# LayerNorm with GELU: the rows of two buffers interleaved in HBM, partitions 64 KB apart instead of 32 KB

## The chip, the cores and the metric

The kernel runs on one core of one Trainium2 chip. The metric is the device time of one execution in microseconds (us); the median over runs is quoted. Runs of this kernel agree to about 0.2%. The profile shows the span of the core's work, which is 1.8 to 1.9 us shorter than the device time. MB and GB/s are in millions and billions of bytes, except where a transfer is called "4 MB": that is 4096 KB.

## The reference

```python
# x: (8, 1024, 2048) float32; gamma, beta: (2048,)
mean = np.mean(x, axis=-1, keepdims=True)
var = np.var(x, axis=-1, keepdims=True)
out = gamma * (x - mean) / np.sqrt(var + eps) + beta
return 0.5 * out * (1 + np.tanh(np.sqrt(2 / np.pi) * (out + 0.044715 * out ** 3)))
```

So 8192 rows of 8 KB go in and 8192 rows of 8 KB come out, 67.1 MB each way. Each row is worked on alone; which rows share a buffer is free to choose, as long as input and output agree.

## The kernel before

Rows go through five SBUF buffers of 128 partitions x 4 rows. The kernel makes 16 such groups: SyncE issues the loads, ScalarE the stores, and a load into a buffer waits until the store out of it has landed. VectorE computes statistics (L148) and the product with gamma (L164), ScalarE normalizes (L201) and does the GELU (L208), TensorE adds beta by matmuls into PSUM, GpSimd takes the power for the standard deviation.

```python
xg = xf.rearrange("(b p r) d -> b p r d", p=P, r=R)      # R = 4 rows, P = 128, 16 groups b
og = of.rearrange("(b p r) d -> b p r d", p=P, r=R)
...
for b in range(B):                                       # SyncE
    s = slot(b)
    if stored(b):
        sy.wait_ge(s_store[s], stored(b))                # the buffer's store has landed
    for q in range(R):
        if b == 0:                                       # first group: row by row
            sy.dma_start(out=xts[s][:, q:q + 1], in_=xg[0, :, q:q + 1]).then_inc(s_first[q], 16)
    if b:
        sy.dma_start(out=xts[s], in_=xg[b]).then_inc(s_load[s], 16)
...
ac.dma_start(out=og[b], in_=xt)._wait_ge(s_r, b + 1).then_inc(s_store[slot(b)], 16)   # ScalarE
# the last group is stored row by row (og[b, :, q:q + 1])
```

A group is one solid 4 MB of HBM: partition p has its 32 KB (4 rows), and the 32 KB of partition p + 1 follow at once.

Of the kernel before, what the change touches and what calls it, by code (L numbers as in the profile page):

```python
# [10 lines left out]
R = 4  # L11
# [5 lines left out]
def kernel(  # L17
# [9 lines left out]
    P = 128  # L27
    xf = x.flatten_outer_dims()
    of = out.flatten_outer_dims()
    n, d = xf.shape  # L30
# [3 lines left out]
    T = n // P  # L34
    B = T // R
    assert (B - 1) % SLOTS == 0
    xg = xf.rearrange("(b p r) d -> b p r d", p=P, r=R)
    og = of.rearrange("(b p r) d -> b p r d", p=P, r=R)

    bf16 = mybir.dt.bfloat16  # L40
    f32 = mybir.dt.float32
# [4 lines left out]
    def sb(name, shape, dt):  # L46
        return pool.tile(shape, dt, name=name)

    xts = [sb(f"xt{s}", [P, R, d], f32) for s in range(SLOTS)]
# [17 lines left out]
    def sem(name):  # L67
        return tc.alloc_semaphore(name)

    s_first = [sem(f"first{q}") for q in range(R)]  # L70
# [17 lines left out]
    def slot(b):  # L88
        return (b + SLOTS - 1) % SLOTS

    def row(p):
        return rows[p:p + 1, :, :d // K]

    def split(v):
        return v.rearrange("o (k f) -> o k f", k=K)
# [4 lines left out]
    def by_row(b):  # L100
        return b == B - 1

    def stored(b):
        return sum(16 * (R if by_row(c) else 1) for c in range(b) if slot(c) == slot(b))

    with tc.tile_critical(no_gpsimd_drain=True):  # L106
        with nc.Block(no_gpsimd_drain=True) as block:

            @block.sync
            def _(sy):  # L110
                for b in range(B):
                    s = slot(b)
                    if stored(b):
                        sy.wait_ge(s_store[s], stored(b))
                    for q in range(R):
                        if b == 0:
                            sy.dma_start(out=xts[s][:, q:q + 1], in_=xg[0, :, q:q + 1]).then_inc(s_first[q], 16)
                    if b:
                        sy.dma_start(out=xts[s], in_=xg[b]).then_inc(s_load[s], 16)

# [67 lines left out]
            @block.scalar  # L188
            def _(ac):
                ac.preload_act_table(ACT.Gelu_apprx_tanh)  # L190
                for k, (p, src) in enumerate(((64, gamma), (0, beta), (32, beta))):
                    ac.dma_start(out=row(p), in_=src.rearrange("(o k f) -> o k f", o=1, k=K)).then_inc(s_par[k], 16)
                ac.wait_ge(s_m, 1)
                ac.activation(out=split(b_hl[0:1]), in_=row(0), func=ACT.Identity)._wait_ge(s_par[1], 16).then_inc(s_c, 1)  # L194
                ac.activation(out=split(b_hl[32:33]), in_=row(32),  # L195
                              func=ACT.Identity)._wait_ge(s_par[2], 16).then_inc(s_c, 1)
                ac.activation(out=g_t, in_=pss[0], func=ACT.Identity)._wait_ge(s_tg, 1).then_inc(s_c, 1)  # L197
                for t in range(T + 1):
                    if t < T:
                        b, q = divmod(t, R)  # L200
                        ac.activation(out=yks[t % 2], in_=xts[slot(b)][:, q], func=ACT.Identity, scale=rss[:, q:q + 1],  # L201
                                      bias=nms[:, q:q + 1])._wait_ge(s_p, t + 1).then_inc(s_n, 1)
                    i = t - 1
                    if i < 0:
                        continue
                    b, q = divmod(i, R)
                    xt = xts[slot(b)]
                    ins = ac.activation(out=xt[:, q], in_=pss[i % 2], func=ACT.Gelu_apprx_tanh)._wait_ge(s_t, i + 1)  # L208
                    if by_row(b):
                        ins.then_inc(s_r, 1)  # L210
                        ac.dma_start(out=og[b, :, q:q + 1], in_=xt[:, q:q + 1])._wait_ge(  # L211
                            s_r, b + q + 1).then_inc(s_store[slot(b)], 16)
                        ac.sem_inc(s_g, 1)
                    elif q == R - 1:
                        ins.then_inc(s_r, 1)
                        ac.dma_start(out=og[b], in_=xt)._wait_ge(s_r, b + 1).then_inc(s_store[slot(b)], 16)  # L216
                        ac.sem_inc(s_g, 1)
                    else:
                        ins.then_inc(s_g, 1)
# [69 lines left out]
```

## Time and profile before

| | before |
|---|---|
| device time, median | 319.68 us |
| span in the profile | 317.8 us |
| busiest compute engine | VectorE, 265.0 us (83%) |
| the two DMA queues, share of 16 engines | 49.4% and 49.1% |
| bytes moved | 134.27 MB |
| rate in the middle of the run | 431 to 433 GB/s |

Read it in this order: no compute engine is full, the DMA engines are, and the stretch table shows whether their rate ever sags. The prediction below shows the lines.

### The profile page before, as it was taken

What the parts mean: (1) busy time and instruction counts of PE and PEld (TensorE: products, weight loads), DVE (VectorE), ACT (ScalarE), POOL (GpSimd) and SP (SyncE); (2) the same over time, 40 slices, a digit from 0 to 9 for tenths busy, and PEclk for the clock granted to TensorE, in tenths of its full rate; (3) what the DMA queues carried; (4) which work ended last, traced back from release to release, by engine and by line L of the source; (5) the groups of instructions that cost most, each with busy time, mean ns of one, the idle gap of its engine ahead of it and who ended that gap; (6) DMA issues with size and microseconds to landing.
All of it is one profiled execution on the core that took longest, in us unless ns stands there. A gap on an engine that the chain in (4) does not pass through costs nothing.

```text
span 317.8 us, 2075 instructions
## 1 busy us (share of the span) xinstructions
PE 244.3 (77%) x520; PEld 57.1 (18%) x520; DVE 265.0 (83%) x514; ACT 253.9 (80%) x132; POOL 79.0 (25%) x73
## 2 busy tenths in 40 slices
PE   2769988888888898888877868598595895868810
PEld 1211222111212122211111111122121111112100
DVE  3499999999999999999969799696996969879500
ACT  2679999999999999999969779696995969968920
POOL 1033323232323231323213222231312213212000
DMA  7999999999999999999999999999999999999994
GB/s 291 438 462 396 459 396 445 412 454 404 458 400 459 422 437 445 412 450 408 458 417 441 437 421 454 404 458 412 450 433 425 450 408 450 408 458 421 437 404 206
DMA packets 5571, 134.27 MB, mean 423 GB/s; under 512 B 656, under 2 KB 704, under 8 KB 704
## 3 DMA queue, kind: packets, MB, share of 16 engines
q1 hardware_dynamic: 2736, 67.11, 49.4%
q10 hardware_dynamic: 2832, 67.13, 49.1%
q14 instruction: 3, 0.02, 0.0%
HBM read 67.13 MB, written 67.11 MB: 422 GB/s over the span
## 4 chain that ended last, share of the span: by engine, by line
DMA 44%; DVE 27%; ACT 19%; PE 3%; issue 2%; ACTq 1%; DVEq 0%; SPq 0%
DMA out_dram<-xt 27%; DVE sts L148 15%; DMA xt<-in_x_dram 15%; ACT yk L201 12%; DVE zg L164 9%; ACT xt L208 7%; PE ps L226 2%; DMA rows<-in_gamma_dram 2%; DVE mvs L157 2%; DVE nms L141 1%; ACTq L216 1%; DVE ves L158 1%; PE ps L243 1%; ACT g_t L197 1%; ACTq L211 0%
## 5 line engine op out<-in xcount | busy, mean ns | idle before, releaser
L148 DVE BATCH_NORM_STATS2 sts<-xt 128x6 f32<-128x512 f32 x256 | 163.5, 681 | 23.7 <-DMA xt<-in_x_dram 21.7
L201 ACT ACTIVATE yk<-xt,nms,rss 128x2048 bf16<-128x2048 f32 x64 | 134.1, 2095 | 41.7 <-DVE nms L141 41.2
L243 PE MATMUL ps<-zg,ident 128*128 128x512 bf16 x256 | 120.8, 627 | 50.9 <-DVE zg L164 50.9
L132 POOL TENSOR_TENSOR rss<-ves,mhalf 128x1 f32<-128x1 f32 x64 | 78.0, 1219 | 216.5 <-DVE ves L158 157.0
L239 PE MATMUL ps<-b_hl,ones_b 33*128 33x512 bf16 x256 | 120.6, 624 | 2.2 <-PEq L234 2.2
L208 ACT ACTIVATE xt<-ps 128x2048 f32<-128x2048 f32 x64 | 118.8, 1857 | 1.5 <-PE ps L243 1.5
L164 DVE TENSOR_TENSOR zg<-yk,g_t 128x2048 bf16<-128x2048 bf16 x64 | 78.0, 1218 | 5.0 <-ACT yk L201 3.0
L243 PEld LDWEIGHTS ps<-zg,ident 128*128 128x128 bf16 x256 | 27.6, 130 | 144.1 <-DVE zg L164 108.7
L239 PEld LDWEIGHTS ps<-b_hl,ones_b 33*128 33x128 bf16 x256 | 27.0, 127 | 92.1 <-issue 88.4
L157 DVE BATCH_NORM_AGGREGATE mvs<-sts 128x2 f32<-128x24 f32 x64 | 16.9, 264 | 2.2
L141 DVE TENSOR_SCALAR nms<-mvs,rss 128x1 f32<-128x1 f32 x64 | 12.6, 196 | 0.0
L226 PE MATMUL ps<-rows,ones 1*128 1x512 f32 x8 | 7.2, 1072 | 6.0 <-DMA rows<-in_gamma_dram 6.0
L158 DVE TENSOR_SCALAR ves<-mvs 128x1 f32<-128x1 f32 x64 | 9.8, 154 | 2.2
L194 ACT ACTIVATE b_hl<-rows 1x2048 bf16<-1x2048 f32 x1 | 1.9, 1909 | 4.9 <-DMA rows<-in_beta_dram 4.9
L226 PEld LDWEIGHTS ps<-rows,ones 1*128 1x128 f32 x8 | 2.5, 323 | 9.2 <-DMA rows<-in_gamma_dram 6.0
L172 DVE TENSOR_TENSOR b_hl<-rows,b_hl 1x2048 bf16<-1x2048 f32 x1 | 2.3, 2281 | 2.1 <-ACT b_hl L195 2.1
L197 ACT ACTIVATE g_t<-ps 128x2048 bf16<-128x2048 f32 x1 | 1.9, 1877 | 2.4 <-PE ps L226 2.4
L190 ACT ACT_TABLE_LOAD x1 | 1.3, 1283 | 0.9 <-SPq L106 0.9
L167 DVE MEMSET b_hl<- 33x1024 uint32 x1 | 0.9, 912 | 1.2 <-SPq L106 1.2
L195 ACT ACTIVATE b_hl<-rows 1x2048 bf16<-1x2048 f32 x1 | 1.9, 1908 | 0.0
L123 POOL MEMSET ones<- 65x128 f32 x1 | 0.2, 202 | 0.5 <-SPq L106 0.5
L127 POOL TENSOR_SCALAR_AFFINE_SELECT ident<-ident 128x128 bf16<-128x128 bf16 x1 | 0.3, 294 | 0.1
(7 smaller groups left out, 0.9 us busy)
## 6 DMA issues: line engine op xcount, KB each, us to landing
xt<-in_x_dram SPq DMA_DIRECT2D x15, 4096.0 KB, 24.3
out_dram<-xt ACTq DMA_DIRECT2D x15, 4096.0 KB, 37.0
xt<-in_x_dram SPq DMA_DIRECT2D x4, 1024.0 KB, 8.1
out_dram<-xt ACTq DMA_DIRECT2D x4, 1024.0 KB, 12.7
rows<-in_beta_dram ACTq DMA_DIRECT2D x2, 8.0 KB, 5.6
rows<-in_gamma_dram ACTq DMA_DIRECT2D x1, 8.0 KB, 5.0
```

Of the source, the lines that this page charges most:

```text
L132: po.tensor_tensor(out=rss[:, c], in0=ves[:, c], in1=mhalf, op=ALU.pow)._wait_ge(s_a, k + 1).then_inc(s_q, 1)
L141: ve.tensor_scalar(out=nms[:, c], in0=mvs[:, q, 0:1], scalar1=rss[:, c], scalar2=-1.0, op0=ALU.mult, op1=ALU.mult)._wait_ge(s_q, count).th ...
L148: ins = ve.bn_stats(out=sts[:, q, j, :], in_=xr[:, j, :])
L157: ve.bn_aggr(out=mvs[:, q], in_=sts[:, q])._wait_ge(s_o, count + 1).then_inc(s_o, 1)
L158: ve.tensor_scalar(out=ves[:, q:q + 1], in0=mvs[:, q, 1:2], scalar1=float(eps), scalar2=1.0, op0=ALU.add, op1=ALU.mult)._wait_ge(s_o, coun ...
L164: ve.tensor_tensor(out=zgs[q % 2], in0=yks[q % 2], in1=g_t, op=ALU.mult)._wait_ge(s_n, count).then_inc(s_z, 1)
L197: ac.activation(out=g_t, in_=pss[0], func=ACT.Identity)._wait_ge(s_tg, 1).then_inc(s_c, 1)
L201: ac.activation(out=yks[t % 2], in_=xts[slot(b)][:, q], func=ACT.Identity, scale=rss[:, q:q + 1], bias=nms[:, q:q + 1])._wait_ge(s_p, t + ...
L208: ins = ac.activation(out=xt[:, q], in_=pss[i % 2], func=ACT.Gelu_apprx_tanh)._wait_ge(s_t, i + 1)
L226: ins = pe.matmul(pss[0][:, cols(j)], lhsT=ones[64:65], rhs=rows[64:65, j * K // nsub:(j + 1) * K // nsub, :d // K], start=True, stop=True)
L239: ins = pe.matmul(ps[:, cols(j)], lhsT=ones_b, rhs=b_hl[:, cols(j)], start=True, stop=False)
L243: ins = pe.matmul(ps[:, cols(j)], lhsT=ident, rhs=zgs[k % 2][:, cols(j)], start=False, stop=True)
```

## The change

The intent: let two consecutive groups share 8 MB of HBM. A partition owns eight consecutive rows (64 KB); the even group takes the first four, the odd group the last four. Each transfer still moves 128 runs of 32 KB, but they start 64 KB apart, so a transfer touches every second 32 KB of 8 MB.

```diff
-    xg = xf.rearrange("(b p r) d -> b p r d", p=P, r=R)
-    og = of.rearrange("(b p r) d -> b p r d", p=P, r=R)
+
+    def groups(v):
+        v = v.rearrange("(g p c r) d -> g c p r d", p=P, c=2, r=R)
+        return [v[b // 2, b % 2] for b in range(B)]
+
+    xg, og = groups(xf), groups(of)
...
-  ... in_=xg[0, :, q:q + 1]
+  ... in_=xg[0][:, q:q + 1]
...
-  ... out=og[b, :, q:q + 1]
+  ... out=og[b][:, q:q + 1]
```

More of the change, by code (lines that the diff above doesn't have):

```diff
@@ L116, in _ @@
                         if b == 0:
-                            sy.dma_start(out=xts[s][:, q:q + 1], in_=xg[0, :, q:q + 1]).then_inc(s_first[q], 16)
+                            sy.dma_start(out=xts[s][:, q:q + 1], in_=xg[0][:, q:q + 1]).then_inc(s_first[q], 16)
                     if b:
@@ L210, in _ @@
                         ins.then_inc(s_r, 1)
-                        ac.dma_start(out=og[b, :, q:q + 1], in_=xt[:, q:q + 1])._wait_ge(
+                        ac.dma_start(out=og[b][:, q:q + 1], in_=xt[:, q:q + 1])._wait_ge(
                             s_r, b + q + 1).then_inc(s_store[slot(b)], 16)
```

## The prediction

The sum came to 319.68 + 0 + about 0.1 = 319.8 us, in a range of 318.8 to 321.5. The about 0.1 is the guess at a cost of the new pitch. Rival 1 asks whether a transfer that touches every second 32 KB is served by only half of HBM, rival 2 whether a loss grows with the pitch.

> **What bounds the kernel now.** I read the page's busy shares first. No compute engine is full: VectorE has the most, 83% of the span, then ScalarE 80% and TensorE 77%.
>
> ```profile
> span 317.8 us, 2075 instructions
> PE 244.3 (77%) x520; PEld 57.1 (18%) x520; DVE 265.0 (83%) x514; ACT 253.9 (80%) x132; POOL 79.0 (25%) x73
> ```
>
> Then I read the slices and the queues of the same page. The DMA row is at 9 (90% or more) in 38 of 40 slices, and the two queues that carry loads (q1) and stores (q10) together take 49.4 + 49.1 = 98.5% of the sixteen DMA engines' time.
>
> ```profile
> DMA  7999999999999999999999999999999999999994
> DMA packets 5571, 134.27 MB, mean 423 GB/s; under 512 B 656, under 2 KB 704, under 8 KB 704
> q1 hardware_dynamic: 2736, 67.11, 49.4%
> q10 hardware_dynamic: 2832, 67.13, 49.1%
> ```
>
> Third, the stretch table (windows), whose last two columns are the DMA share and GB/s. It tells whether the DMA engines are always fed and at what rate.
>
> ```profile
> 0.00:1.00 1.00, 0.00 (x0) 0.00 (x0) 0.00 (x0) 0.10 (x1) 0.26 (x5) 1.00 0.00 0
> 1.00:2.00 1.00, 0.00 (x0) 0.00 (x0) 0.77 (x1) 1.00 (x1) 0.76 (x5) 1.00 0.15 33
> 2.00:3.00 1.00, 0.00 (x0) 0.00 (x0) 0.14 (x1) 0.19 (x1) 0.00 (x0) 1.00 0.84 197
> ...
> 80.00:120.00 40.00, 35.40 (x78) 8.23 (x77) 39.09 (x78) 37.10 (x20) 12.80 (x10) 1.00 1.00 431
> 160.00:200.00 40.00, 30.58 (x67) 6.87 (x65) 34.04 (x66) 32.14 (x18) 10.88 (x9) 1.00 1.00 433
> 240.00:280.00 40.00, 30.92 (x68) 7.12 (x67) 32.80 (x64) 30.85 (x16) 9.87 (x8) 1.00 1.00 432
> 300.00:318.00 18.00, 2.73 (x6) 0.43 (x4) 1.23 (x1) 3.81 (x3) 0.00 (x0) 1.00 0.75 319
> ```
>
> The share is 1.00 in the middle, whether VectorE is nearly full (39.09 of 40 us in 80:120) or not (32.80 in 240:280), and the rate stays at 431 to 433 GB/s. In the second half the engines do less per microsecond because they wait for data. So this is a transfer-bound program, whose compute runs ahead until about 137 us and is then paced by the landings. The chain of waits says the same: in its second half it hops from a store that frees a buffer to the load that fills it.
>
> ```profile
> 136.65 41.68 DMA out_dram<-xt
> 178.34 24.18 DMA xt<-in_x_dram
> ...
> 211.47 44.27 DMA out_dram<-xt
> 255.76 24.20 DMA xt<-in_x_dram
> ```
>
> From these the span is rebuilt in three terms. Body: 134.27 MB at 432 GB/s = 310.8 us. Head: the first five microseconds moved at 0, 33, 197, 410 and 420 GB/s, 1.06 MB where 2.16 MB would fit, so 1.10 MB are missing = 2.55 us. Tail: 300:318 moved 319 x 18 = 5.74 MB where 7.78 MB would fit, 2.03 MB missing = 4.7 us. Sum 318.05 us, against a span of 317.8. The device time is 319.68, so 1.9 us lie outside the span and I carry them over. What sets the time is therefore one number, the rate at which sixteen always-busy DMA engines move bytes; each 1% of it is worth 3.1 us.
>
> [...]
>
> **The change part by part.** The order of the instructions, set against the kernel before, is the same on every engine but for line numbers: the same loads, stores, waits, arithmetic and semaphores. All that moves is addresses in HBM.
> - Large transfers: 30 of 4 MB (15 each way). A partition still reads or writes one unbroken run of 4 rows x 2048 x 4 B = 32 KB. Before, the next partition's run followed at once (a transfer is one solid 4 MB); now the next one begins 64 KB on (a transfer is every second 32 KB of 8 MB). Packets: 15 x 128 = 1920 each way, no more and no smaller. Work added on a DMA engine: none, 0 us.
> - Small transfers: 4 + 4 of 1 MB, by row: 8 KB runs, 64 KB apart where they were 32 KB apart. Again 512 packets each way as before: 0 us.
> - Rows change places between buffers, in the same manner for x and for out, so the result is the same and each buffer is still 4 MB.
> - What could cost is only how HBM answers[...] and it counts in full on the path if it occurs, since the engines have no idle share to hide it in. [...]
> Sum: 319.68 + 0 + about 0.1 = 319.8 us.
>
> **Rivals.**
> 1. *The transfer touches half of the memory.* One of the two buffers uses only the even 32 KB pieces, the other only the odd ones. [...] Against it is the kernel's own end: its last four stores each write 8 KB out of every 32 KB, a quarter of the addresses, and yet while only they run the rate holds:
>
> ```profile
> 305.00:310.00 5.00, 0.00 (x0) 0.00 (x0) 0.00 (x0) 0.29 (x1) 0.00 (x0) 1.00 1.01 426
> ```
>
> So leaving out three quarters of the 8 KB pieces costs at most (432 - 426) / 432 = 1.4% of rate, with the start of the drain in it. [...] That doesn't prove it for the 32 KB piece[...]. Also, a load and a store in flight together may be of different parity. Chance 2%.
> 2. *A mild aliasing of engines that go in step.* The engines' starting points also move twice as far apart[...]. Chance 3% of over 2%, and perhaps 10% of a few tenths of a percent.
> 3. *Faster.* Two neighbouring buffers now share an 8 MB region, which might suit HBM better. [...] Faster by over 2% is under 313.3 us, so a body of 304.4 us and 441 GB/s. Chance 1%.
> 4. *A later landing starves an engine.* If one DMA engine fell behind, a load would land later and VectorE, which waits 21.7 us for loads in 8 places, would wait longer. But all engines get the same number of packets as before, and VectorE's 52.8 us of idle time lie off the bound. It moves the time only through a later last load, by tenths of a microsecond.
>
> ```profile
> DVE sts L148 <- DMA xt<-in_x_dram: 21.7, 8, 3.7
> ```
>
> **Range and chances.** [...] Runs before differ by 0.08 us, so noise adds nothing. Faster 0.01, slower 0.02 + 0.03 = 0.05, within 2% 0.94.
>
> **What would show it.** Right: the two queues' packets at 2736 and 2832 and their shares within half a point of 49.4% and 49.1%; 430 to 433 GB/s in the middle stretches at a DMA share of 1.00; loads of 4 MB landing after about 24 us and stores after about 37; VectorE, ScalarE and TensorE busy times unchanged to 1%; the chain ending in the same four stores. Rivals 1 and 2 would show as the same DMA share of 1.00 at a lower rate[...]. [...] Rival 4 would show the DMA share under 1.00 with longer waits for loads. I am wrong if the rate in the middle leaves 428 to 435 GB/s, above all if it falls while the share stays at 1.00: then HBM is the bound at this pitch[...].

## The result

| | before | after |
|---|---|---|
| device time, median | 319.72 us (319.67 to 320.09, 4 runs) | 319.68 us (319.65 to 319.79, 4 runs) |
| ratio after / before | | 0.9997, 95% interval 0.9982 to 1.0012 |
| last 4 MB load lands | 280.0 us | 280.4 us |
| span | 317.8 us | 317.9 us |

A ratio here is the mean time of one kernel's runs over the mean of the other's runs of the same rounds, so it is not quite the ratio of the medians. The interval leaves room for 0.2% either way.

The page of the kernel after, busy shares and queues (queue: packets, MB, share of sixteen engines):

```profile
span 317.9 us, 2075 instructions
PE 244.4 (77%) x520; PEld 57.3 (18%) x520; DVE 265.0 (83%) x514; ACT 253.8 (80%) x132; POOL 79.0 (25%) x73
...
q1 hardware_dynamic: 2736, 67.11, 49.5%
q10 hardware_dynamic: 2832, 67.13, 49.0%
```

Same packets, same bytes, shares moved by 0.1 of a point. The stretch table of the kernel after (stretch, busy time of each engine, TensorE clock, DMA share, GB/s):

```profile
80.00:120.00 40.00, 35.42 (x78) 8.28 (x77) 39.09 (x78) 37.05 (x20) 12.78 (x10) 1.00 1.00 433
160.00:200.00 40.00, 30.97 (x68) 7.13 (x66) 34.04 (x68) 32.17 (x18) 10.43 (x9) 1.00 1.00 433
240.00:280.00 40.00, 30.95 (x68) 7.13 (x67) 32.78 (x64) 30.85 (x16) 9.86 (x8) 1.00 1.00 433
300.00:318.00 18.00, 3.15 (x7) 0.57 (x5) 1.23 (x1) 4.23 (x3) 0.00 (x0) 1.00 0.77 326
```

In these three stretches the rate is 433 GB/s at a share of 1.00, where it was 431, 433 and 432. One earlier stretch, 40 to 80 us, has 425 at a share of 0.98 against 431 at 1.00, but 120 to 160 us has 434 against 433, and the last load still lands within 0.4 us of before. That early stretch differs from run to run and not with the pitch: it has 431 at 256 KB, and 431 in another run at 64 KB (e2_even_then_odd). The chain of waits (start, length, what) is the same hop from store to load to store:

```profile
136.59 40.54 DMA out_dram<-xt
177.16 25.81 DMA xt<-in_x_dram
...
211.92 43.31 DMA out_dram<-xt
255.25 25.14 DMA xt<-in_x_dram
```

A store is about 1 us shorter and a load 1 to 1.6 us longer than before, in each pair; the sums are 66.4 and 68.5 us against 65.9 and 68.5. The two queues share the engines (49.5% and 49.0% of their time), so what one gives the other takes. The runs below show the same shuffle with no change of the total (the two loads of the chain took 24.4 and 25.2 us in e2_even_then_odd and 26.3 and 25.6 us in e10_pitch256k, at 319.76 and 319.64 us), so it isn't a cost of the pitch.

### The profile page after: what moved, and what is told of

It reads as the page before. It is cut to its first block, busy times and chain, and to the rows that moved or that the text cites. A ratio compares the mean times of both kernels' runs of the same rounds, so it can differ in the third digit from the quotient of the medians.

```text
span 317.9 us, 2075 instructions
## 1 busy us (share of the span) xinstructions
PE 244.4 (77%) x520; PEld 57.3 (18%) x520; DVE 265.0 (83%) x514; ACT 253.8 (80%) x132; POOL 79.0 (25%) x73
## 3 DMA queue, kind: packets, MB, share of 16 engines
q1 hardware_dynamic: 2736, 67.11, 49.5%
## 4 chain that ended last, share of the span: by engine, by line
DMA 44%; DVE 27%; ACT 19%; PE 3%; issue 2%; ACTq 1%; DVEq 0%; SPq 0%
DMA out_dram<-xt 26%; DMA xt<-in_x_dram 16%; DVE sts L152 15%; ACT yk L205 12%; DVE zg L168 9%; ACT xt L212 7%; PE ps L230 2%; DMA rows<-in_gamma_dram 2%; DVE mvs L161 2%; DVE nms L145 1%; ACTq L220 1%; DVE ves L162 1%; PE ps L247 1%; ACT g_t L201 1%; ACTq L215 0%
## 5 line engine op out<-in xcount | busy, mean ns | idle before, releaser
L152 DVE BATCH_NORM_STATS2 sts<-xt 128x6 f32<-128x512 f32 x256 | 163.4, 680 | 23.7 <-DMA xt<-in_x_dram 22.1
## 6 DMA issues: line engine op xcount, KB each, us to landing
out_dram<-xt ACTq DMA_DIRECT2D x15, 4096.0 KB, 36.5
```

What stands on the lines that cost most here:

```text
L152: ins = ve.bn_stats(out=sts[:, q, j, :], in_=xr[:, j, :])
```

## The experiments

The theory: sixteen always-busy DMA engines set the time by their own rate, and HBM has rate to spare, so where the rows lie in HBM doesn't matter until a layout eats the spare. The rivals: a transfer that is served by only half of HBM, hidden by its neighbours on the other half; an aliasing, that is a loss that grows with the pitch; a time set by compute or waits. All edits below are made to the kernel after, and are printed shortened: lines are joined by a semicolon, and ends of lines such as `.then_inc(...)` are left out. Runs marked "one look" have one time and no interval; the kernel before took 319.86 and 319.69 to 319.71 us beside them.

| run | what | device us | against before |
|---|---|---|---|
| e11_pitch128k | pitch 128 KB | 319.57 | 0.9998 (0.9982 to 1.0015) |
| e10_pitch256k | pitch 256 KB | 319.64 | 1.0007 (0.9990 to 1.0024) |
| e1_pitch512k | pitch 512 KB | 322.65 | 1.0105 (1.0077 to 1.0133) |
| e2_even_then_odd | 64 KB, all even groups first | 319.76 | 1.0003 (0.9987 to 1.0020) |
| e3_rows8k | packets of 8 KB | 322.60 | 1.0090 (1.0073 to 1.0107) |
| e4_store2m | stores 2 MB apart | 339.98 | one look |
| e5_store2m_less4k | stores 2 MB - 4 KB apart | 319.68 | one look |
| e6_same_rows | all partitions load the same 32 KB | 319.94 | one look |
| e7_less_load | 11.5 MB fewer loaded | 297.51 | one look |
| e8_sbuf_source | loads read SBUF, not HBM | 375.74 | one look |
| e9_hbm_to_hbm | stores copy x from HBM | 330.09 | one look |

### Does DMA time lie on the path? (e7_less_load, e3_rows8k)

```diff
-  sy.dma_start(out=xts[s], in_=xg[b])
+  m = R if b < SLOTS else R - 1
+  sy.dma_start(out=xts[s][:, :m], in_=xg[b][:, :m])
```

> Wrong result on purpose: the last eleven loads bring three of a partition's four rows, so 11 MB (11.5 MB in millions of bytes) are not moved; the arithmetic on old data stays the same. Theory (DMA time is on the path in full): body 122.7 / 432 = 284.1 us in place of 310.8, so 293 us if nothing else binds; compute binds first, since VectorE needs 4.12 us for each of 64 row groups from about 15 us on, which ends near 300 us in the device time; so 296 to 304 us. Rival (compute or waits set the time): 319.7 us within 1%.

Measured: 297.51 us, 22 us less. The chain of waits by engine has turned from 44% DMA to 2%:

```profile
DVE 53%; ACT 34%; PE 3%; issue 3%; ACTq 2%; DMA 2%; DVEq 0%; SPq 0%
```

So the transfers did set the time before and after the change, and compute stands about 22 us behind them. Had compute been the bound, a layout could have cost something unseen.

The second run makes each byte a little dearer for the DMA engines, by smaller packets:

```diff
-  v.rearrange("(g p c r) d -> g c p r d", p=P, c=2, r=R);  v[b // 2, b % 2]
+  v.rearrange("(b r p) d -> b p r d", p=P, r=R);  v[b]
```

> Each partition takes four rows 1 MB apart, so a 4 MB transfer is solid again but goes in packets of 8 KB, four times as many. This changes the cost of a byte on the DMA engine, not the load on HBM. In the trace of before the packets of the first and last transfers (8 KB) take about 309 ns and the 32 KB ones 1213 ns, so four small ones take 1236 ns, 1.9% more. Theory (DMA engine time is the bound and is on the path in full): 310.8 x 1.9% = +5.9 us, about 325.6 us. Rival (the time is set by something else, compute or semaphore waits, and the DMA rate has slack): 319.7 us within 0.5%.

Measured: 322.60 us, +2.9 us. The direction is as the theory said and the size is half. The stretch table of this run:

```profile
160.00:200.00 40.00, 30.53 (x68) 6.99 (x66) 33.67 (x68) 31.58 (x17) 9.86 (x8) 1.00 1.01 427
240.00:280.00 40.00, 30.46 (x68) 7.08 (x66) 33.55 (x68) 31.67 (x18) 9.95 (x9) 1.00 1.01 428
```

The rate in the middle, from 80 to 280 us, fell from 432.4 GB/s (the mean of five stretches of before) to 427.8, which is 1.06%; of a body of 310.8 us that is 3.3 us, about what was measured. The 1.9% came from adding packet durations; the share of 1.01 says that the recorded durations of small packets overlap a little, so the sum of four seems to overstate their cost. The sensitivity is as the prediction had it: about 3 us for each 1% of DMA rate, with nothing to absorb it. The edit also moves a partition's four rows 1 MB apart; that the packets cost the time, and not this distance, was not tested apart.

### Does a transfer meet half of HBM? (e2_even_then_odd)

```diff
-  return [v[b // 2, b % 2] for b in range(B)]
+  return [v[b % 8, b // 8] for b in range(B)]
```

The hidden form of rival 1: one transfer is served by half of HBM, but its neighbour or the stores beside it use the other half, so that the change shows nothing.

> The change's 64 KB pitch, but the eight buffers of even 32 KB pieces first and the eight of odd pieces after them, so that for most of the run the loads and the stores in flight together all lie on even pieces, or all on odd ones. Theory: 319.7 us within 0.5%. Rival 1 in its hidden form[...]: both halves can no longer balance, so the middle stretches fall well under 430 GB/s[...].

Measured: 319.76 us, ratio 1.0003. Until about 124 us loads and stores ask only for even 32 KB pieces, and from about 196 us on only for odd ones (between these, loads of odd pieces run beside stores of even ones). The rate is full in both:

```profile
80.00:120.00 40.00, 35.42 (x77) 8.12 (x76) 39.09 (x77) 37.20 (x20) 12.78 (x10) 1.00 1.00 430
200.00:240.00 40.00, 30.55 (x67) 7.18 (x68) 32.78 (x64) 31.20 (x17) 10.14 (x9) 1.00 1.00 433
```

Rival 1 falls, in its hidden form too: leaving out every second 32 KB costs nothing.

### Where does the pitch begin to count? (e11_pitch128k, e10_pitch256k, e1_pitch512k, e4_store2m, e5_store2m_less4k)

Three correct kernels, with 4, 8 and 16 groups sharing a region:

```diff
-  v.rearrange("(g p c r) d -> g c p r d", p=P, c=2, r=R);   v[b // 2, b % 2]
+  v.rearrange("(g p c r) d -> g c p r d", p=P, c=4, r=R);   v[b // 4, b % 4]     # e11, 128 KB
+  v.rearrange("(g p c r) d -> g c p r d", p=P, c=8, r=R);   v[b // 8, b % 8]     # e10, 256 KB
+  v.rearrange("(g p c r) d -> g c p r d", p=P, c=B, r=R);   v[0, b]              # e1, 512 KB
```

> Partitions 512 KB apart in a transfer (sixteen buffers share 64 MB), eight times the pitch of the change; every result is still right and every packet still 32 KB. Theory (the DMA engines' own rate is the bound, HBM has rate to spare): 319.7 us, within 0.5%, and 431 to 433 GB/s in the middle at a DMA share of 1.00. [...]

> Partitions 256 KB apart, eight buffers share 32 MB; the result is right. 512 KB cost 1.05%, 64 KB nothing. If the cost grows with the pitch (rival 2 in a small form), 256 KB lies between: 0.3 to 0.8%, 320.7 to 322.3 us. If it is something of the 512 KB layout alone: 319.7 us within 0.2%.

> Partitions 128 KB apart, four buffers share 16 MB; the result is right. Twice the pitch of the change. Theory: 319.7 us within 0.2%; if the cost halves with each halving of the pitch from 512 KB, +0.26%, 320.5 us.

Measured: 128 KB and 256 KB cost nothing that these rounds can show; 512 KB costs 1.05%, +3 us, and its runs scatter more (321.83 to 323.91 us). So the cost isn't proportional to the pitch, and both forms of "half as much at half the pitch" missed: it starts between 256 and 512 KB. In the profiled run of 512 KB (321.83 us, its fastest) the chain of waits reads:

```profile
136.84 42.60 DMA out_dram<-xt
179.46 26.62 DMA xt<-in_x_dram
...
215.04 41.86 DMA out_dram<-xt
256.91 26.63 DMA xt<-in_x_dram
```

The first load of this chain lands at 206.1 us, where it landed at 203.0 after the change, and the last one at 283.5 against 280.4: 3 us were lost before 206 us and not again. From the last load to the end it takes 36.5 us against 37.5, so this run's span is only 2.1 us longer. Its rate is 420 GB/s from 40 to 80 us (425 after the change) and 430 to 433 from there to 280 us, so it isn't a loss spread evenly over the run. The slower runs were not profiled, and why the time is lost stays open.

To see a layout hurt, the stores were sent to a scratch tensor with its partitions 2 MB apart, and then 4 KB nearer:

```diff
-  xg, og = groups(xf), groups(of)
+  xg = groups(xf)
+  pitch = 524288                    # e4: 2 MB of float32;  e5: 524288 - 1024
+  wide = nc.dram_tensor("wide", (P, pitch), mybir.dt.float32).ap()
+  og = [wide[:, b * R * d:(b + 1) * R * d].rearrange("p (r d) -> p r d", r=R) for b in range(B)]
```

> Wrong result on purpose: all stores go to a scratch tensor in HBM whose partitions lie exactly 2 MB apart; the output is left unwritten. Loads as in the change. Theory: HBM's spare rate is finite, and at such a pitch it should run out. [...] Rival (layout never matters on this chip at any pitch): 319.7 us within 0.5%.

> Wrong result on purpose, like the run with stores 2 MB apart, but each partition 4 KB nearer: 2,093,056 bytes apart in the scratch tensor. If the 20 us that the 2 MB pitch cost came from addresses that agree in their low bits, they go: 319.7 us within 0.5%, last stores landing after about 12.5 us again. If they came from the size of the region or from the scratch tensor as such, they stay: about 340 us.

Measured: 339.98 us and 319.68 us. The 4 KB restore everything, so it is the exact pitch that costs, not the scratch tensor or its size. The cost is 20 us. The stretch table of the 2 MB run shows where it lies:

```profile
40.00:80.00 40.00, 35.69 (x78) 8.38 (x79) 39.17 (x78) 36.95 (x20) 11.33 (x9) 1.00 0.99 378
160.00:200.00 40.00, 29.14 (x65) 6.63 (x63) 32.31 (x65) 30.37 (x17) 9.87 (x8) 1.00 1.00 422
...
305.00:310.00 5.00, 4.29 (x10) 1.14 (x11) 4.29 (x10) 4.38 (x3) 0.55 (x1) 1.00 0.97 419
...
320.00:325.00 5.00, 0.00 (x0) 0.00 (x0) 0.00 (x0) 0.00 (x0) 0.00 (x0) 1.00 1.00 213
```

While the first stores run beside loads (40 to 80 us) the rate is 378 GB/s, against 425 after the change, and from 80 to 280 us it is 413 to 426 against 432 to 434. Together this makes the last load land at 267.30 + 24.97 = 292.3 us, 12 us late. From there on only stores run, and as long as their pieces are of 32 KB they still move at 419 (423 after the change, from 290 to 300 us): stores alone are not what suffers. The fall to 213 comes with the last four stores, which go row by row in pieces of 8 KB (in the trace the first of these starts at about 313 us); after the change the same pieces ran at 423. So from the last load to the end it takes 45.9 us against 37.5. Why pieces of 8 KB lose half and pieces of 32 KB only a little, at one and the same pitch, stays open.

### Is the limit in HBM or before it? (e6_same_rows, e8_sbuf_source, e9_hbm_to_hbm)

```diff
+  xg = [xf[b * R:(b + 1) * R].rearrange("(o r) d -> o r d", o=1).broadcast_to((P, R, d)) for b in range(B)]
```

The rival here is that it doesn't matter where HBM is read.

> Wrong result on purpose: in every load all 128 partitions read the same 32 KB of x (four rows), so the sixteen engines ask for one small place of HBM at a time; packets and bytes are as in the change. It asks whether HBM's spare rate is spare everywhere. Theory (HBM's spare rate lies in its spread over many places): loads slow down, the rate falls under 400 GB/s at a share near 1.00, the time is above 340 us. Rival[...]: 319.7 us within 0.5%.

Measured: 319.94 us beside 319.86 of before. My expectation missed: sixteen engines reading one and the same 32 KB are served as fast as reads over 4 MB, at 432 or 433 GB/s from 80 to 280 us. How HBM serves a repeated place was not looked into, so this run says less about spread than I had wanted; it does say that 432 GB/s needs no spread of the reads.

```diff
-  sy.dma_start(out=xts[s], in_=xg[b])
+  sy.dma_start(out=xts[s], in_=held.broadcast_to((P, R, d)))     # held: a [128, 1, 2048] tile in SBUF, set once
```

> Wrong result on purpose: the fifteen big loads copy 8 KB pieces of a tile in SBUF four times over and read no HBM; stores as in the change. Packets of loads are 8 KB, as in the run with rows 1 MB apart, which cost +2.9 us for both directions. Theory (the limit is on the near side, not in HBM): the loads take as long as HBM loads of 8 KB packets, q1 near 49.8% of the engines' time, about 321 us. Rival (HBM reads or the mix of reads and writes in HBM set 432 GB/s): the loads' share falls below 47% or the rate exceeds 440 GB/s, and the time falls below 313 us.

Measured: 375.74 us, a miss on both sides: without HBM reads the transfers became slower. The queue lines of this run:

```profile
q1 hardware_dynamic: 8496, 67.11, 54.4%
q10 hardware_dynamic: 2832, 67.13, 42.6%
```

The run had more than one change in it: loads go in packets of 8 KB and start later, behind the setting of `held`, and they now read SBUF as the stores do, so SBUF was read for both queues. 4 MB loads took 65.0 us to land, and from 80 to 280 us the rate was 343 to 370 GB/s. It can't tell HBM's limit from the engines', and is inconclusive. The opposite swap is cleaner, since it loads HBM more and SBUF less:

```diff
-  ac.dma_start(out=og[b], in_=xt)
+  ac.dma_start(out=og[b], in_=xg[b])      # and the same for the row-wise stores
```

> Wrong result on purpose: every store copies x itself from HBM to HBM in place of the finished tile from SBUF, at the same moments, in the same sizes and with the change's pitch (the output is x). HBM then carries 201 MB in place of 134 (reads double), while the DMA engines move what they moved. Theory (DMA engines bind, HBM has rate to spare): 319.7 us within 1%, shares of q1 and q10 near 49%. Rival (HBM's own rate, read and write together, is what 432 GB/s is): 201.4 MB at 432 GB/s = 466 us for the body, about 475 us.

Measured: 330.09 us. HBM carried half as much again, and the page and the stretch table show where that was felt:

```profile
HBM read 134.24 MB, written 67.11 MB: 613 GB/s over the span
```

```profile
160.00:200.00 40.00, 32.30 (x71) 7.27 (x68) 35.37 (x70) 33.52 (x18) 10.53 (x9) 1.00 1.00 433
240.00:280.00 40.00, 30.82 (x68) 7.04 (x67) 32.79 (x64) 30.85 (x16) 9.87 (x8) 1.00 1.00 432
280.00:300.00 20.00, 14.90 (x34) 3.49 (x34) 16.60 (x33) 16.25 (x9) 4.02 (x4) 1.00 1.01 339
300.00:318.00 18.00, 3.64 (x8) 0.73 (x6) 1.23 (x1) 4.90 (x3) 0.00 (x0) 1.00 0.95 314
```

From 80 to 280 us the DMA engines move 431 to 433 GB/s as ever, half loads and half copies, so HBM reads and writes about 216 + 2 x 216 = 648 GB/s there without slowing anything. No transfer reads SBUF there, and the rate is the same, so reads of SBUF don't set 432 GB/s either; whether it is the engines themselves or the paths to them, no run separates. Only after the last load (at 280.5 us), when every engine copies from HBM to HBM and would want 2 x 432 = 864 GB/s at HBM, does the rate fall to 339 and 314, that is 678 and 628 GB/s at HBM. That HBM's total gives out here, and not something else in a copy, is likely but wasn't tested apart. The extra 10 us lie in that tail: 47.8 us from the last load's landing to the end, where the kernel after needs 37.5. The rival's 475 us is out, and so is the theory's "within 1%" for the whole, which had not thought of the tail.

## Why the prediction was right

**The bound.** It held that one number sets the time, the rate of sixteen always-busy DMA engines. Confirmed: fewer bytes took 22 us off until compute took over (e7), and 1% of rate cost about 3 us (e3).

**HBM's spare rate.** The copy run (e9) shows a spare: 648 GB/s at HBM with no loss in the middle, and 678 over 20 us of the tail. The kernel draws 432 of it.

**Added work 0.** The packets and bytes of both queues and the instruction count are the same; busy times agree to 0.1 us at VectorE, ScalarE and TensorE.

**The pitch's cost, about 0.1 us.** Measured -0.03% with an interval of 0.2% on both sides. The estimate scaled a loss assumed for 512 KB, which no run had shown, down by the pitch. The scale was unneeded and its form wrong: 512 KB costs 1.05%, and 256 KB nothing that its rounds can show (1.0007, 0.9990 to 1.0024).

**Rival 1** fell in e2. **Rival 2** fell in the result, and in e11 and e10 at two and four times its pitch; e4 and e5 show a cost at 2 MB (20 us) that 4 KB less pitch takes away, and e1 a small one (1.05%) at 512 KB whose cause is open. **Rival 3** (faster) did not show: the middle stretches ran at 431 to 433 GB/s before and 432 to 434 after. **Rival 4** would have been a share under 1.00 with longer waits for loads: from 80 to 280 us the share isn't under 1.00, and VectorE waits 22.1 us for loads where it waited 21.7.

**What was off.** Loads were to land after about 24 us; the median was 26.0, with stores a little shorter in exchange. It costs nothing. The prediction also called itself wrong if the rate in the middle left 428 to 435 GB/s; its three middle stretches stayed at 433, but 40 to 80 us had 425, which cost no time: the bounds were too narrow for a stretch that early.

## What to carry to other kernels

When the DMA engines are full at a steady rate and the rate doesn't depend on what else goes on, ask on which side of them the limit lies before you move data about in memory: here HBM gave 648 GB/s in the copy run (e9) and the kernel draws 432, and none of the pitches of 32, 64, 128 and 256 KB could be told from the others (ratios to 32 KB of 0.9997, 0.9998 and 1.0007). A pitch of 2 MB, in one run, cost 1 to 5% of the rate in pieces of 32 KB once the stores were under way (413 to 426 GB/s from 80 to 280 us, against 432 to 434), and half of it in pieces of 8 KB (213 against 423); 4 KB less pitch undid both (319.68 us, 432 or 433 GB/s from 80 to 280 us, 429 from 305 to 310 us). So where rows must lie at such a pitch, look first at the transfers with small pieces, here the row-wise stores at the end.
